# Compressed probabilities in pairs, 512-column scores, later additions and another loading of the first tiles, in a hybrid decoder layer

## The chip, the cores and the metric

The kernel runs on one core of a Trainium2 chip. The metric is the device time of one execution in microseconds, median over runs. The core has five engines with instruction streams of their own: TensorE (PE, with weight loads shown apart as PEld), VectorE (DVE), ScalarE (ACT), GpSimd (POOL) and SyncE (SP, which here only issues DMAs).

## The reference

One decoder layer on 512 tokens of width 1024: a pooling mixer and an attention with compressed and windowed keys side by side, merged by sigmoid gates, then a gated conv-MLP. What matters here, cut down:

```python
h = rms_norm(x, mix_norm_g)
u, q, kv, nsa_g, merge_g = split(h @ w_in)            # pool input, queries, 6 key/value slots, gates
gate_pool, gate_nsa = split(sigmoid(merge_g))
y_pool = pooling_mixer(u, pool_w, pool_scale) @ w_pool_out   # running means over 2, 4, 8, 16 tokens
# attention, per head h (8 heads, 2 key groups): three branches, each a softmax
#   compressed: 31 blocks of 32 tokens, through a small MLP: blk = kv[:, idx] + cmp_pe; silu(blk @ w1) @ w2
#   selected and windowed: with 512 tokens both see every earlier token
out = g0 * (p_cmp @ vc) + g1 * (p_sel @ v_sel) + g2 * (p_win @ v_win)
x = x + (gate_pool * y_pool + gate_nsa * (out @ w_nsa_out)) @ w_out
h = rms_norm(x, ffn_norm_g)
gate_pre, val = split(h @ w_up)
x = x + (silu(causal_dwconv(gate_pre)) * val) @ w_down
```

## The kernel before

Every float32 product is made of three products of rounded halves (high by high, high by low, low by high), so most weights and activations are split by a rounding copy on ACT and a subtraction on DVE, or by a DMA from POOL's queue that adds. The program isn't written in its final order: each call is recorded, and a planner (`Plan`, emitted at one line, so that every row of the profile reads L395) puts the instructions of each engine in order from its own costs and due times. PE work is recorded in two streams: `m` (the main one: projection, rotary transposes, compression, attention) and `f` (the filler: 22 "features", each 24 matmuls of 512 columns on `xh`, `xl` with weights `wf`, then the pool mixer's output products). The planner takes from `f` where `m` has to wait, so the order of `f` is free to be chosen.

The stages in time: `first()` and `round_a` (the projection to queries and keys: tiles `tr`, `av`, `sc` <- `whi`, `xh`), values (`bh`, `bl`), rotary rope and the transposes of queries and keys (`qs`, `ks` into `qt`, `kt`), compression (`kcb`, `w1`, `hid`, `kcsp`, `kcz`), attention head by head, `wno`, `wout`, then the MLP (`wup`, `wdn`, `wdz`).

The steps that the change touches:

- **The beginning.** Ten float32 matmuls of `ones` come first on PE. ACT issues the load of a small parameter tile `pr`, then does one dummy activation `warm`, which loads its table. SP issues, in this order: half of the first weights (`raw[:, :T]`), both halves of the first x tile `xr[0]`, the rest of the weights. ACT rounds the weights, then each half of x to `xh[0]`; DVE makes `xl[0]` from both halves.
- **Key transposes** (`qk_transpose`). For each block t of 128 tokens, eight transposes of queries and four of keys; three ACT copies make two layouts `KT[0, t]`, `KT[1, t]`.
- **Scores** (`scores(h, i)`). For head h and query block i there are n = i + 1 key blocks; each takes two matmuls (high and low halves of the keys) of 256 columns, 20 per head:

```python
for j in range(n):
    for s in range(2):
        PE.matmul(pt[:, j], QT[g, i][:, hh], KT[s, j][:, g], ...)
```

- **Compressed branch.** `cmp_softmax(g)` makes probabilities in three parts (high, low, high) of 32 columns in `cst`; `cmp_transpose(g, i)` transposes 96 columns of each head of group g, four transposes for each of eight (g, i); `av` multiplies them by `vst` (96 rows, 64 columns). The addition `blk + cmp_pe` (tiles `kcb` <- `kc`) is done by POOL, four times on 128x512.
- **The order of `f`.** First the two compressed features (`kv_in`: tiles `kc`), then `pool_in` and gates by turns; `mix(gi)` (three matmuls `mm<-pmh,pwh`, `mm<-pml,pwh`, `mm<-pmh,pwl`) follows one feature after the `pool_in` that it needs.

Of the kernel before, what the change touches and what calls it, by code (L numbers as in the profile page):

```python
# [2 lines left out]

# [12 lines left out]
P = 128  # L16
T = 512
# [381 lines left out]
def hybrid_layer(ctx: ExitStack, tc: tile.TileContext, xT, pos, par, cst, poolw, w1, wa, wb, wf,  # L399
# [9 lines left out]
    def f32(ap):  # L409
        return ap.bitcast(F32)  # L410
# [12 lines left out]
    def bank(tag, shape=(P, T)):  # L423
        return pl.tile(ps, shape, F32, tag, tag, {"mm": 2, "tr": 3, "av": 1, "sc": 1}[tag], psum=True)
# [66 lines left out]

    POOL.memset(ones, 1.0)
    ACT.dma_start(pr[:, 0:16], par[:, 0:16])
    ACT.activation(warm, ones[:, 0:1], AF.Square)
    pt = bank("mm")
    for i in range(10):
        PE.matmul(pt[:, 0:P], ones, ones, start=(i == 0), stop=(i == 9))

    xr, xh, xl = [None] * KD, [None] * KD, [None] * KD
    acc = page("acc")  # L500
# [10 lines left out]
    def first():  # L511
        raw, hi, low = ring("wraw"), ring("whi", F32R), ring("wlo", F32R)
        xr[0] = page("xr")
        xh[0], xl[0] = page("xh", dt=F32R), page("xl", dt=F32R)
        cuts = (slice(0, H2), slice(H2, T))
        with pl.unit():
            SP.dma_start(raw[:, :T], wa[0, :, :T])
            for c in cuts:
                SP.dma_start(xr[0][:, c], xT[0, :, c])
            SP.dma_start(raw[:, T:768], wa[0, :, T:768])  # L520
        ACT.activation(hi[:, :T], raw[:, :T], AF.Copy)
        for c in cuts:
            with pl.behind(pl.last()):
                ACT.activation(xh[0][:, c], xr[0][:, c], AF.Copy, scale=mixg[:, 0:1])
        with pl.behind(pl.last()):
            ACT.activation(hi[:, T:768], raw[:, T:768], AF.Copy)
        DVE.scalar_tensor_tensor(xl[0], xr[0], mixg[:, 0:1], f32(xh[0]), op0=ALU.mult, op1=ALU.subtract)
        DVE.tensor_sub(low[:, :768], raw[:, :768], f32(hi[:, :768]))
        for t in range(NT):
            PE.matmul(psq[t], xh[0][:, t * P:(t + 1) * P], hi[:, 0:512], start=True, stop=False)  # L530
        for t in range(NT):
            PE.matmul(pskt[:, t // 2, t % 2], xh[0][:, t * P:(t + 1) * P], hi[:, 512:768], start=t % 2 == 0, stop=False,
                      skip_group_check=True)
        wak[0] = hi, low
# [172 lines left out]
    def qk_transpose(t):  # L707
        for g in range(2):
            pt = bank("tr", (P, 4, P))
            with pl.unit():  # L710
                for i in range(4):
                    PE.transpose(pt[:, i], f32(qsp[t][g][:, i].rearrange("p a d -> p (a d)")), ident)
            QT[g, t] = page("qt", (P, 4, P), F32R)
            ACT.activation(QT[g, t], pt, AF.Copy)
        pt = bank("tr", (P, 2, 2, P))
        with pl.unit():
            for g in range(2):
                for b in range(2):
                    PE.transpose(pt[:, g, b], f32(ksp[t][:, 2 * b + g].rearrange("p a d -> p (a d)")), ident)
        KT[0, t], KT[1, t] = (page("kt", (P, 2, 2, P), F32R) for _ in range(2))  # L720
        ACT.activation(KT[0, t], pt, AF.Copy)
        ACT.activation(KT[1, t][0:64], pt[64:128], AF.Copy)
        ACT.activation(KT[1, t][64:128], pt[0:64], AF.Copy)

    rope_split(0)
    rope_split(1)
# [19 lines left out]
    pscale = R("pscale")  # L746
    yph, ypl, pooled = [], [], {}
    with pl.on("f"):
        for i in range(2):
            pt = feature(i, xh, xl)  # L750
            kc = page("kc", (P, 2, 256))
            for g in range(2):
                for q in range(2):
                    DVE.tensor_mul(kc[q * 64:(q + 1) * 64, g], pt[g * 64:(g + 1) * 64, q::2],
                                   rb[g * 64:(g + 1) * 64, q::2])
            for a in range(2):
                b = page("kcb", (P, 2, 32, 8))
                POOL.tensor_add(b.rearrange("p g n l -> p (g n) l"), kc.rearrange("p g (n l) -> p (g n) l", l=8),
                                pe[:, i, 8 * a:8 * a + 8][:, None, :].to_broadcast([P, 64, 8]))
                KC[i, a] = b  # L760
        def pool_in(gi):
            w = 2 << gi
# [36 lines left out]
        def pool_out(c):  # L799
            wh, wl = weights(wpo[c].rearrange("p a k n -> p (a k n)"), 1024)  # L800
            for f in (2 * c, 2 * c + 1):
# [3 lines left out]
                DVE.scalar_tensor_tensor(gpy[f], gpy[f], 1.0, pt, op0=ALU.add, op1=ALU.mult)  # L805
                SP.dma_start(gdr[f], gpy[f])

        pool_in(0)
        pw = page("pw", (P, 4, P))
        with pl.behind(turned[1]):  # L810
            SP.dma_start(pw, poolw)
        split(pwh, pwl, pw)
        for gi in range(1, 4):
            pool_in(gi)
            gate(thn, gi - 1, 14)
            mix(gi - 1)
        gate(thn, 3, 14)
        mix(3)
        for f in (0, 2):
            gate(gpy, f, 6)  # L820
            gate(gpy, f + 1, 6)
            pool_out(f // 2)
        gate(thn, 4, 14)
        for f in (4, 6):
            gate(gpy, f, 6)
            gate(gpy, f + 1, 6)
            pool_out(f // 2)
        for f in range(5, 8):
            gate(thn, f, 14)

    chid = []
    for i in range(2):
# [40 lines left out]
        for z in kcz.values():  # L873
            POOL.memset(f32(z), 0.0)
    pk = compress_out(1)
    vst = keep("vst", (96, 2, DH), F32R)
    for g in range(2):
        src = pk[g * 32:(g + 1) * 32, 0:64]
        for s in range(2):
            ACT.activation(vst[s * 32:(s + 1) * 32, g], src, AF.Copy, scale=0.5)  # L880
        DVE.scalar_tensor_tensor(vst[64:96, g], src, 0.5, f32(vst[g * 32:(g + 1) * 32, g]),
                                 op0=ALU.mult, op1=ALU.subtract)

    def compress_kt():
        pt = bank("tr")
# [11 lines left out]
    cps, cst_ = {}, {}  # L897
    PTc = {g: pl.tile(sb, (96, 4, T), F32R, "ptc", "ptc", 1) for g in range(2)}

    def cmp_scores(g):  # L900
        pt = bank("tr")
# [8 lines left out]
    def cmp_softmax(g):  # L910
        pt = bank("tr", (P, 4, P))
        with pl.unit():
            for hh in range(4):
                PE.transpose(pt[:, hh], cps[g][:, hh], ident)
        e = page("ce", (P, 16, 32))
        e4 = e.rearrange("p (h t) n -> p h (t n)", h=4)
        sm = keep("csm", (P, 3, 16), bufs=2)
        st = cst_[g] = keep("cst", (P, 16, 3, 32), F32R)
# [12 lines left out]
    def cmp_transpose(g, i):  # L931
        pt = bank("tr", (P, 4, P))
        with pl.unit():
            for hh in range(4):
                PE.transpose(pt[0:96, hh], f32(cst_[g][:, 4 * hh + i].rearrange("p a n -> p (a n)")), ident)
        ACT.activation(PTc[g][:, :, i * P:(i + 1) * P], pt[0:96], AF.Copy)

    Pt, PT, po, Oraw = {}, {}, {}, {}
    Oh = [page("oh", dt=F32R) for _ in range(4)]
# [2 lines left out]
    def scores(h, i):  # L942
# [1 line left out]
        n = i + 1  # L944
        pt = bank("sc", (P, 4, 2, P)) if n > 2 else bank("tr", (P, 2, 2, P))
        with pl.unit():
            for j in range(n):
                for s in range(2):
                    PE.matmul(pt[:, j], QT[g, i][:, hh], KT[s, j][:, g], start=(s == 0 and j % 2 == 0),
                              stop=(s == 1), skip_group_check=True)  # L950
# [79 lines left out]
    cmp_softmax(0)  # L1030
    scores(0, 2)
    scores(0, 3)
    extra = {(0, 2 * i + 2): (lambda i=i: cmp_transpose(0, i)) for i in range(NT)}
    extra.update({(4, 2 * i): (lambda i=i: cmp_transpose(1, i)) for i in range(NT)})
    extra[2, 6] = lambda: cmp_softmax(1)
    for h in range(H):
        def nxt(i):
# [396 lines left out]
```

## Time and profile before

| | |
|---|---|
| median of 3 runs | 698.51 us (698.43 to 698.52) |
| the profiled execution | 698.77 us, of which 697.0 us are the span of its instructions |
| PE busy | 691.3 us, 4144 matmuls |
| DVE, ACT, POOL busy | 481.1, 436.3, 103.3 us |
| granted TensorE clock | 1.0 |

Matmuls are pipelined: the duration of a row (0.39 us for 512 columns) is longer than the distance from one start to the next, and it is the distance that sets the pace. Rows of the timeline give the start, the time until the last of a group ends, the engine, the operation, the tile that is written `<-` the tiles that are read, and in brackets the idle time before it with what ended it.

### The profile page before, as it was taken

How to read it: one execution, taken by the hardware profiler on the slowest of the kernel's cores; microseconds unless marked ns; L12 is line 12 of the kernel's file. 1: busy time of each engine (PE TensorE's matmuls, PEld its weight loads, DVE VectorE, ACT ScalarE, POOL GpSimd, SP SyncE). 2: the span in 40 equal slices, each digit the busy share in tenths (PEclk: the TensorE clock that was granted, in tenths of full speed). 3: DMA queues.
4: the chain of work that ended last, by engine and by line, in shares of the span. 5: the costliest groups of instructions: out<-in, count | busy, mean ns of one | idle time of the engine just before them, and what ended most of it. 6: DMA issues, size and time to landing. Idle time of an engine off the chain costs nothing.

```text
span 697.0 us, 11326 instructions
## 1 busy us (share of the span) xinstructions
PE 691.3 (99%) x4144; PEld 612.0 (88%) x4144; DVE 481.1 (69%) x1025; ACT 436.3 (63%) x798; POOL 103.3 (15%) x127
## 2 busy tenths in 40 slices
PE   9999999999999999999999999999999999999998
PEld 8898888888888888888888899999999999999987
DVE  5768678888866653685559977777766766776542
ACT  7667568767777663443359757768677766675320
POOL 0011400010011010000013223223122112220000
PEclk9999999999999999999999999999999999999999
DMA  8577344355655558744459787879978867864141
GB/s 297 171 177 207 96 111 107 106 137 122 166 136 152 151 126 240 272 164 136 151 144 233 168 214 174 215 169 198 225 189 180 196 162 168 182 158 108 46 128 61
DMA packets 45703, 113.99 MB, mean 164 GB/s; under 512 B 5328, under 2 KB 6096, under 8 KB 45648
## 3 DMA queue, kind: packets, MB, share of 16 engines
q1 hardware_dynamic: 29664, 76.57, 34.2%
q0 software_dynamic: 15840, 36.71, 29.2%
q8 instruction: 32, 0.52, 0.3%
q14 instruction: 23, 0.19, 0.1%
q10 hardware_dynamic: 144, 0.01, 0.0%
HBM read 70.27 MB, written 6.29 MB: 110 GB/s over the span
## 4 chain that ended last, share of the span: by engine, by line
PE 97%; DVE 2%; issue 0%; ACT 0%; POOL 0%; POOLq 0%
PE mm L395 41%; PE tr L395 31%; PE sc L395 14%; PE av L395 11%; DVE kp L395 1%; DVE kc L395 0%; DVE qp L395 0%; DVE th L395 0%; DVE qs L395 0%; DVE rt L395 0%; DVE ks L395 0%; DVE pml L395 0%; DVE o L395 0%; ACT ks L395 0%; POOL ones L395 0%
## 5 line engine op out<-in xcount | busy, mean ns | idle before, releaser
L395 ACT ACTIVATE whi<-wraw 128x1024 fp32r<-128x1024 f32 (+2 forms) x97 | 98.0, 1011 | 69.5 <-issue 24.6
L395 DVE TENSOR_TENSOR wlo<-wraw,whi 128x1024 fp32r<-128x1024 f32 (+1 forms) x66 | 76.3, 1158 | 16.9 <-ACT whi L395 14.9
L395 POOL DMA_DIRECT2D wlo<-wraw x30 | 26.3, 876 | 327.5 <-ACT wlo L395 257.9
L395 PE MATMUL mm<-xh,whi 128*128 128x512 f32 x176 | 73.0, 415 | 0.1
L395 PE MATMUL mm<-xh,wlo 128*128 128x512 f32 x176 | 69.0, 392 | 0.0
L395 PE MATMUL mm<-xl,whi 128*128 128x512 f32 x176 | 68.9, 392 | 0.0
L395 PE MATMUL mm<-tl,sh 128*128 128x256 f32 x190 | 53.5, 282 | 0.0
L395 PE MATMUL mm<-th,sl 128*128 128x256 f32 x174 | 49.1, 282 | 0.0
L395 PE MATMUL mm<-th,sh 128*128 128x256 f32 x174 | 49.0, 281 | 0.0
L395 ACT ACTIVATE wlo<-wraw 128x1024 fp32r<-128x1024 f32 x30 | 31.8, 1059 | 25.5 <-PE mm L395 16.6
L395 POOL DMA_DIRECT2D sl<-r x36 | 31.1, 863 | 88.0 <-ACT sl L395 66.1
L395 ACT ACTIVATE pp<-pp,asm 128x128 f32<-128x128 f32 (+3 forms) x64 | 35.4, 556 | 9.4 <-DVE asm L395 9.3
L395 PE MATMUL sc<-yh,whi 128*128 128x512 f32 x104 | 40.5, 389 | 0.0
L395 PE MATMUL sc<-yl,whi 128*128 128x512 f32 x104 | 40.5, 389 | 0.0
L395 PE MATMUL sc<-yh,wlo 128*128 128x512 f32 x104 | 40.5, 389 | 0.0
L395 PEld LDWEIGHTS mm<-xh,wlo 128*128 128x128 f32 x176 | 33.0, 188 | 7.5
L395 DVE SCALAR_TENSOR_TENSOR ft<-fg,pr,ft 128x511 f32<-128x511 f32 (+1 forms) x44 | 32.9, 749 | 9.5 <-ACT ft L395 8.8
L395 PEld LDWEIGHTS mm<-xh,whi 128*128 128x128 f32 x176 | 33.2, 188 | 4.7 <-DVE th L395 0.5
L395 PEld LDWEIGHTS mm<-xl,whi 128*128 128x128 f32 x176 | 33.3, 189 | 4.0
L395 PEld LDWEIGHTS mm<-tl,sh 128*128 128x128 f32 x190 | 35.7, 188 | 0.4
L395 PEld LDWEIGHTS mm<-th,sh 128*128 128x128 f32 x174 | 32.7, 188 | 1.1
L395 PEld LDWEIGHTS mm<-th,sl 128*128 128x128 f32 x174 | 32.7, 188 | 0.0
(397 smaller groups left out, 2100.6 us busy)
## 6 DMA issues: line engine op xcount, KB each, us to landing
wlo<-wraw POOLq DMA_DIRECT2D x30, 512.0 KB, 4.6
wraw<-wup SPq DMA_DIRECT2D x26, 512.0 KB, 3.9
wraw<-wf SPq DMA_DIRECT2D x22, 512.0 KB, 3.4
r<-wup SPq DMA_DIRECT2D x36, 256.0 KB, 5.4
sl<-r POOLq DMA_DIRECT2D x36, 256.0 KB, 5.4
wraw<-wdn SPq DMA_DIRECT2D x16, 512.0 KB, 3.7
sl<-s POOLq DMA_DIRECT2D x18, 256.0 KB, 5.5
sl<-wraw POOLq DMA_DIRECT2D x18, 256.0 KB, 4.2
```

The lines of the kernel that those rows point to most:

```text
L395: getattr(self.real[o.eng], method)(*a, **kw)
```

## The change

- `first()`: eight matmuls of `ones` instead of ten. The second half of `xr[0]` is issued by ACT, after `pr` and before the table load; the first weights are rounded by DVE instead of ACT, and the first half of x no longer stands behind that.
- Key transposes are done for two blocks at once, per group; `KT[s, pair, g]` holds two blocks side by side, and scores use 512 columns for a pair of blocks, 256 for a single one: 12 matmuls per head.
- `cmp_softmax` makes two parts (high, low) instead of three; two heads stand side by side in 128 columns, so four calls of `cmp_transpose` of four transposes instead of eight. `PTc` holds head pairs; the values `vz` (128 rows, 128 columns, zero rows for the other head of the pair) share a tile with the probabilities.
- `kcb` is added by DVE, and stands behind the last key copy (`turned[3]`).
- `f` begins with a gate, `mix` comes one `pool_in` and two gates later, and the pool's outputs come last.

```diff
-    ACT.activation(warm, ones[:, 0:1], AF.Square)
-    for i in range(10):
+    for i in range(8):
...
             SP.dma_start(raw[:, :T], wa[0, :, :T])
-            for c in cuts:
-                SP.dma_start(xr[0][:, c], xT[0, :, c])
+            SP.dma_start(xr[0][:, cuts[0]], xT[0, :, cuts[0]])
             SP.dma_start(raw[:, T:768], wa[0, :, T:768])
-        ACT.activation(hi[:, :T], raw[:, :T], AF.Copy)
+        ACT.dma_start(xr[0][:, cuts[1]], xT[0, :, cuts[1]])
+        ACT.activation(warm, ones[:, 0:1], AF.Square)
+        DVE.tensor_copy(hi[:, :T], raw[:, :T])
         for c in cuts:
-            with pl.behind(pl.last()):
+            with pl.behind(pl.last()) if c.start else nullcontext():
                 ACT.activation(xh[0][:, c], xr[0][:, c], AF.Copy, scale=mixg[:, 0:1])
...
+        for g in range(2 if t % 2 else 0):
+            pt = bank("tr", (P, 2, 2, P))
+            with pl.unit():
+                for j in range(2):
+                    for b in range(2):
+                        PE.transpose(pt[:, j, b], f32(ksp[t - 1 + j][:, 2 * b + g]...), ident)
+            hl, lh = (page("kt", (P, 2, 2, P), F32R) for _ in range(2))
+            KT[0, t // 2, g], KT[1, t // 2, g] = hl, lh
...
-                POOL.tensor_add(b..., kc..., pe...)
+                with pl.behind(turned[3]):
+                    DVE.tensor_add(b..., kc..., pe...)
...
+        gate(thn, 0, 14)
+        kv_in(0)
+        kv_in(1)
+        gate(thn, 1, 14)
         pool_in(0)
...
+        gate(thn, 2, 14)
+        gate(thn, 3, 14)
+        pool_in(1)
+        mix(0)
...
-        ACT.activation(st[:, :, 0], e, AF.Copy)
-        ACT.activation(st[:, :, 2], e, AF.Copy)
-        DVE.tensor_sub(st[:, :, 1], e, f32(st[:, :, 0]))
+        ACT.activation(hi, e, AF.Copy)
+        DVE.tensor_sub(lo, e, f32(hi))
...
+    def cmp_transpose(g, b):
+            for q in range(2):
+                for a in range(2):
+                    PE.transpose(pt[:, q, a], f32(cst_[:, 2 * b + a, 2 * q:2 * q + 2]...), ident)
...
-            for j in range(n):
+            for j in range(0, n, 2):
+                m = min(2, n - j)
                 for s in range(2):
-                    PE.matmul(pt[:, j], QT[g, i][:, hh], KT[s, j][:, g], start=(s == 0 and j % 2 == 0),
+                    PE.matmul(pt[:, j:j + m], QT[g, i][:, hh], KT[s, j // 2, g][:, 0:m], start=(s == 0), stop=(s == 1),
...
-            PE.matmul(o[0:64], vst[:, g], PTc[g][:, h % 4], start=False, stop=False)
+            PE.matmul(o, vz[:, g, h % 2].rearrange("p s d -> p (s d)"), PTc[:, h // 2], start=False, stop=False)
```

More of the change, by code (lines that the diff above doesn't have):

```diff
@@ L1 @@
 import math
-from contextlib import ExitStack, contextmanager
+from contextlib import ExitStack, contextmanager, nullcontext
 import concourse.bass as bass
@@ L493, in hybrid_layer @@
     ACT.dma_start(pr[:, 0:16], par[:, 0:16])
-    ACT.activation(warm, ones[:, 0:1], AF.Square)
     pt = bank("mm")
-    for i in range(10):
-        PE.matmul(pt[:, 0:P], ones, ones, start=(i == 0), stop=(i == 9))
+    for i in range(8):
+        PE.matmul(pt[:, 0:P], ones, ones, start=(i == 0), stop=(i == 7))
     xr, xh, xl = [None] * KD, [None] * KD, [None] * KD
@@ L714, in qk_transpose @@
             ACT.activation(QT[g, t], pt, AF.Copy)
[L715 to L723, printed above, removed]
+        for g in range(2 if t % 2 else 0):
[3 more added lines that the diff above has]
+                    for b in range(2):
+                        PE.transpose(pt[:, j, b], f32(ksp[t - 1 + j][:, 2 * b + g].rearrange("p a d -> p (a d)")), ident)
+            hl, lh = (page("kt", (P, 2, 2, P), F32R) for _ in range(2))
+            KT[0, t // 2, g], KT[1, t // 2, g] = hl, lh
+            ACT.activation(hl, pt, AF.Copy)
+            ACT.activation(lh[0:64], pt[64:128], AF.Copy)
+            ACT.activation(lh[64:128], pt[0:64], AF.Copy)
     rope_split(0)
@@ L748, in hybrid_layer, with kv_in @@
     with pl.on("f"):
-        for i in range(2):
+        def kv_in(i):
             pt = feature(i, xh, xl)
@@ L757, in hybrid_layer @@
                 b = page("kcb", (P, 2, 32, 8))
-                POOL.tensor_add(b.rearrange("p g n l -> p (g n) l"), kc.rearrange("p g (n l) -> p (g n) l", l=8),
-                                pe[:, i, 8 * a:8 * a + 8][:, None, :].to_broadcast([P, 64, 8]))
+                with pl.behind(turned[3]):
+                    DVE.tensor_add(b.rearrange("p g n l -> p (g n) l"), kc.rearrange("p g (n l) -> p (g n) l", l=8),
+                                   pe[:, i, 8 * a:8 * a + 8][:, None, :].to_broadcast([P, 64, 8]))
                 KC[i, a] = b
@@ L812, in hybrid_layer @@
         split(pwh, pwl, pw)
[L813 to L816, printed above, removed]
+        gate(thn, 2, 14)
         gate(thn, 3, 14)
-        mix(3)
[L819 to L829, printed above, removed]
+        pool_in(1)
+        mix(0)
+        gate(thn, 4, 14)
+        gate(thn, 5, 14)
+        pool_in(2)
+        mix(1)
+        gate(thn, 6, 14)
+        gate(thn, 7, 14)
+        pool_in(3)
+        mix(2)
+        gate(gpy, 0, 6)
+        gate(gpy, 1, 6)
+        mix(3)
+        pool_out(0)
+        gate(gpy, 2, 6)
+        gate(gpy, 3, 6)
+        pool_out(1)
+        gate(gpy, 4, 6)
+        gate(gpy, 5, 6)
+        pool_out(2)
+        gate(gpy, 6, 6)
+        gate(gpy, 7, 6)
+        pool_out(3)
     chid = []
@@ L875, in hybrid_layer @@
     pk = compress_out(1)
-    vst = keep("vst", (96, 2, DH), F32R)
+    ct = keep("cst", (P, 3, T), F32R)
+    cst_ = ct[:, 0:2].rearrange("p a b -> p (a b)").rearrange("p (t h s n) -> p t h s n", t=4, h=4, s=2)
+    vz = ct[:, 2].rearrange("p (g r s d) -> p g r s d", g=2, r=2, s=2)
+    with pl.behind(turned[2]):
+        POOL.memset(f32(ct[:, 2]), 0.0)
     for g in range(2):
         src = pk[g * 32:(g + 1) * 32, 0:64]
[L879 to L882, printed above, removed]
+        for r in range(4):
+            ACT.activation(vz[r * 32:(r + 1) * 32, g, r // 2, 0], src, AF.Copy, scale=0.5)
+        for r in range(2):
+            DVE.scalar_tensor_tensor(vz[r * 64:r * 64 + 32, g, r, 1], src, 0.5, f32(vz[g * 32:(g + 1) * 32, g, 0, 0]),
+                                     op0=ALU.mult, op1=ALU.subtract)
     def compress_kt():
@@ L895, in compress_kt @@
                                AF.Copy)
-    cps, cst_ = {}, {}
-    PTc = {g: pl.tile(sb, (96, 4, T), F32R, "ptc", "ptc", 1) for g in range(2)}
+    cps = {}
+    PTc = pl.tile(sb, (P, 4, T), F32R, "ptc", "ptc", 1)
     def cmp_scores(g):
@@ L917, in cmp_softmax @@
         sm = keep("csm", (P, 3, 16), bufs=2)
-        st = cst_[g] = keep("cst", (P, 16, 3, 32), F32R)
+        hi, lo = (cst_[:, :, :, s].rearrange("p t h n -> p h t n") for s in range(2))
         DVE.tensor_add(e4, pt, C("cmask")[:, None, :].to_broadcast([P, 4, P]))
@@ L926, in cmp_softmax @@
         DVE.tensor_mul(e, e, sm[:, 2][:, :, None].to_broadcast([P, 16, 32]))
-        ACT.activation(st[:, :, 0], e, AF.Copy)
-        ACT.activation(st[:, :, 2], e, AF.Copy)
-        DVE.tensor_sub(st[:, :, 1], e, f32(st[:, :, 0]))
-    def cmp_transpose(g, i):
-        pt = bank("tr", (P, 4, P))
+        e = e.rearrange("p (h t) n -> p h t n", h=4)
+        ACT.activation(hi, e, AF.Copy)
+        DVE.tensor_sub(lo, e, f32(hi))
+    def cmp_transpose(g, b):
+        pt = bank("tr", (P, 2, 2, P))
         with pl.unit():
-            for hh in range(4):
-                PE.transpose(pt[0:96, hh], f32(cst_[g][:, 4 * hh + i].rearrange("p a n -> p (a n)")), ident)
-        ACT.activation(PTc[g][:, :, i * P:(i + 1) * P], pt[0:96], AF.Copy)
+            for q in range(2):
+                for a in range(2):
+                    PE.transpose(pt[:, q, a], f32(cst_[:, 2 * b + a, 2 * q:2 * q + 2].rearrange("p h s n -> p (h s n)")), ident)
+        ACT.activation(PTc[:, 2 * g:2 * g + 2, 2 * b * P:2 * (b + 1) * P], pt.rearrange("p q a t -> p q (a t)"), AF.Copy)
     Pt, PT, po, Oraw = {}, {}, {}, {}
@@ L946, in scores @@
         with pl.unit():
-            for j in range(n):
+            for j in range(0, n, 2):
+                m = min(2, n - j)
                 for s in range(2):
-                    PE.matmul(pt[:, j], QT[g, i][:, hh], KT[s, j][:, g], start=(s == 0 and j % 2 == 0),
-                              stop=(s == 1), skip_group_check=True)
+                    PE.matmul(pt[:, j:j + m], QT[g, i][:, hh], KT[s, j // 2, g][:, 0:m], start=(s == 0), stop=(s == 1),
+                              skip_group_check=True)
         sm = keep("asm", (P, 4, 2), bufs=4)
@@ L1032, in hybrid_layer @@
     scores(0, 3)
-    extra = {(0, 2 * i + 2): (lambda i=i: cmp_transpose(0, i)) for i in range(NT)}
-    extra.update({(4, 2 * i): (lambda i=i: cmp_transpose(1, i)) for i in range(NT)})
+    extra = {(0, 4 * b + 2): (lambda b=b: cmp_transpose(0, b)) for b in range(2)}
+    extra.update({(4, 4 * b): (lambda b=b: cmp_transpose(1, b)) for b in range(2)})
     extra[2, 6] = lambda: cmp_softmax(1)
```

## The prediction

> **What bounds the kernel now.** I read the page's busy times and chain first, then the waits of PE, then the timeline around each place that the change touches.
>
> ```profile
> PE 691.3 (99%) x4144; PEld 612.0 (88%) x4144; DVE 481.1 (69%) x1025; ACT 436.3 (63%) x798; POOL 103.3 (15%) x127
> ```
> ```profile
> PE 97%; DVE 2%; issue 0%; ACT 0%; POOL 0%; POOLq 0%
> ```
> ```profile
> PE tr L395 <- DVE rt L395: 1.3, 1, 1.3
> PE mm L395 <- POOL ones L395: 1.0, 1, 1.0
> ```
> ```profile
> 270.10 14.28 PE mm L395 x63
> ```
>
> PE is busy for 99% of the span and carries 97% of the chain that ended last; in all it waits twice by the view of waits. So each PE instruction that goes is worth its distance to the next start, and work on DVE, ACT and POOL counts only where PE ends up waiting for it. The fifth row, a piece of the chain, shows 63 filler matmuls in one stretch at the end of attention: the main stream finishes with 14 us of filler left, so a main stream that comes somewhat earlier or later is absorbed. From `wno` on, the order of PE's instructions in the built program is the same as before; all of the effect lies ahead of that.
>
> **Probabilities in pairs.** The number of `cst` transposes falls from 32 to 16. A group of four, and what follows it:
>
> ```profile
> 114.15 0.60 PE L395 MATMUL tr<-cs,cst 128*96 128x128 f32 x4
> 114.51 0.47 PE L395 MATMUL mm<-xh,whi 128*128 128x512 f32 x1
> 114.82 0.39 PE L395 MATMUL mm<-xl,whi 128*128 128x512 f32 x1
> ```
>
> Start to start, the group takes 0.36 us and the matmul behind it 0.31 instead of 0.23 (a price that the next part shows): 0.44 us per group. The new groups have 128 rows instead of 96 on the output side; the neighbouring `pp` transposes have 128 as well and I take the same price. Four groups go: −1.76 us. The product with the values keeps 512 columns and its count, so I price it at nothing. On ACT, copies disappear (two per softmax become one, and half of the `ptc` copies go), four small ones are added; nobody on PE waits for these.
>
> **512-column scores.** Per head 20 matmuls become 12: 16 of the 256-column ones become 8 of 512, 64 fewer in all.
>
> ```profile
> 94.42 3.79 PE L395 MATMUL tr<-qt,kcz 128*128 128x512 f32 x16
> 98.05 0.64 PE L395 MATMUL tr<-kt,qt 128*128 128x256 f32 x4
> ```
> ```profile
> 101.74 1.12 PE L395 MATMUL sc<-kt,qt 128*128 128x256 f32 x8
> 102.69 0.40 PE L395 MATMUL mm<-xh,whi 128*128 128x512 f32 x1
> ```
>
> Sixteen of 512 columns take 98.05 − 94.42 = 3.63 us, 0.227 each; eight of 256 take 102.69 − 101.74 = 0.95, 0.119 each. A pair costs 0.238 against 0.227: 0.011 × 64 = −0.7 us. The same columns pass through; only a small cost per instruction goes. Scores of pairs need key copies of both blocks, so the first head's can begin only after the second block's transposes; filler stands between.
>
> **The wait of 1.5 us.** The largest stall is at the query transposes of the fourth block:
>
> ```profile
> 72.08 0.39 PE L395 MATMUL mm<-xh,wlo 128*128 128x512 f32 x1
> 73.81 0.63 PE L395 MATMUL tr<-cs,qs 128*128 128x128 f32 x4 [1.35 <-DVE rt L395]
> ```
> ```profile
> 61.89 0.42 DVE L395 TENSOR_TENSOR kp<-kp,gkv 128x256 f32<-128x256 f32 x1
> ```
> ```profile
> 65.03 1.72 DVE L395 TENSOR_TENSOR kc<-mm,rb 64x256 f32<-64x256 f32 x4
> ```
> ```profile
> 66.79 0.23 DVE L395 TENSOR_TENSOR kp<-kp,rope 128x64 f32<-128x64 f32 x1
> 67.05 1.19 DVE L395 TENSOR_TENSOR kp<-kp,rt 128x64 f32<-128x64 f32 x1
> ```
> ```profile
> 69.21 0.41 DVE L395 TENSOR_TENSOR ks<-kp,ks 128x256 fp32r<-128x256 f32 x1
> ```
> ```profile
> 70.79 2.31 DVE L395 TENSOR_TENSOR kp<-kp,gkv 128x256 f32<-128x256 f32 x1
> ```
> ```profile
> 71.22 1.60 POOL L395 TENSOR_TENSOR kcb<-kc,pr 128x512 f32<-128x512 f32 x1
> ```
> ```profile
> 73.25 0.42 DVE L395 TENSOR_TENSOR qs<-qp,qs 128x256 fp32r<-128x256 f32 x1
> ```
>
> Between two starts lie 1.73 us instead of 0.23: 1.50 lost. The cause stands in DVE's rows: the same multiplication `kp<-kp,gkv` takes 0.42 us alone and 2.31 while POOL adds `kcb`. A smaller one, 128x64, had 1.19 against 0.23 under the addition before. DVE's split `qs`, queued behind both, comes 1.89 + 0.96 us late, and PE waits for it. The change takes POOL's additions away; and the features whose `kc` rows (1.72 us for four) stood ahead in DVE's queue come after a gate now, which puts one 512-column product in there instead. A product of that size is 0.69 by a row quoted next:
>
> ```profile
> 83.60 0.69 DVE L395 TENSOR_TENSOR u<-mm,rb 128x512 f32<-128x512 f32 x1 [1.06 <-PE mm L395]
> ```
> ```profile
> 77.49 1.80 ACT L395 ACTIVATE kt<-tr 128x512 fp32r<-128x512 f32 x3 [0.34 <-PE tr L395]
> ```
>
> DVE therefore gets to `qs` earlier by 1.89 + 0.96 + 1.72 − 0.69 = 3.9 us. PE arrives earlier too: in the built order 51 filler matmuls and 32 transposes stand ahead of that point instead of 60 and 36, 9 × 0.227 + 4 × 0.09 = 2.4 us. So the wait falls by 3.9 − 2.4 = 1.5 us, to nothing, and the built order leaves a margin: it puts the last steps of the third block's keys (0.23, 0.23, 0.41 by the rows) behind `qs` on DVE. I take −1.5, with 0 and −1.5 as ends.
>
> What comes late next is compression. The four `kcb` additions are on DVE now, 0.69 us each, and stand behind the last key copy on ACT. Behind them on DVE are the evictions of the second compressed feature, and PE's first `kcb` matmul waits for the first addition. ACT's copies take 0.60 each; the built order does the one that is waited for first, after PE's last key transposes. So 0.1 + 0.6 + 0.69 = 1.4 us must be covered, and nine filler matmuls, 2.0 us, stand there: no wait. If ACT did all six copies first, 3.6 us, PE would wait 2.3.
>
> **Later additions.** The pool mixer's products wait on DVE's low halves:
>
> ```profile
> 145.44 0.39 PE L395 MATMUL mm<-pmh,pwl 128*128 128x512 f32 x1
> 145.93 0.50 PE L395 MATMUL mm<-xh,whi 128*128 128x512 f32 x1
> ```
> ```profile
> 153.28 0.48 PE L395 MATMUL mm<-pmh,pwh 128*128 128x512 f32 x1
> 153.86 0.50 PE L395 MATMUL mm<-pml,pwh 128*128 128x512 f32 x1
> 154.20 0.39 PE L395 MATMUL mm<-pmh,pwl 128*128 128x512 f32 x1
> ```
>
> Over 0.227 each, these lose 0.26 + 0.35 + 0.11 = 0.7 us. With `mix` two gates later there are over 10 us between; I take −0.5, ends 0 and −0.7, since another order meets its own small waits.
>
> **The beginning.**
>
> ```profile
> 0.99 4.63 PE L395 MATMUL mm<-ones 128*128 128x128 f32 x20 [0.99 <-POOL ones L395]
> ```
> ```profile
> 1.18 0.90 SPq L395 DMA_DIRECT2D xr<-xT  x2
> ```
> ```profile
> 3.65 0.63 ACT L395 ACTIVATE whi<-wraw 128x512 fp32r<-128x512 f32 x1 [0.98 <-DMA wraw<-wa]
> ```
> ```profile
> 4.18 0.49 ACT L395 ACTIVATE xh<-xr,pr 128x256 fp32r<-128x256 f32 x1
> ```
> ```profile
> 5.28 1.74 PE L395 MATMUL tr<-whi,xh 128*128 128x512 f32 x3
> ```
> ```profile
> 5.69 0.51 ACT L395 ACTIVATE xh<-xr,pr 128x256 fp32r<-128x256 f32 x1 [1.02 <-DMA xr<-xT]
> ```
> ```profile
> 6.84 0.41 PE L395 MATMUL av<-whi,xh 128*128 128x512 f32 x1
> 7.09 0.63 PE L395 MATMUL sc<-whi,xh 128*128 128x256 f32 x4
> ```
> ```profile
> 40.80 1.05 PE L395 MATMUL mm<-diag,ones 128*128 128x128 f32 x8
> 41.61 0.38 PE L395 MATMUL mm<-bh,xh 128*128 128x280 f32 x1
> ```
>
> The 20 passes of the ten warm-up matmuls are 0.21 apart (4.29 / 20) and end at 5.28, though `xh` was there at 4.67: the first product waited for the warm-up. Sixteen passes end at 4.4. With DVE rounding weights from 3.65 and ACT free for x, the first product starts at 4.4 to 4.75. The third needs the second half of x, which lands at 5.69 now. Issued from ACT it goes out one issue, 0.45 us, sooner (two on SP take 0.90): the chain from there moves by 0.45. Nearest other bound: it could land with the first half, by 4.18, and then PE's start decides, 0.85. A third bound is below: the same passes are 0.10 apart at 40.80 (0.81 / 8), so PE is at half pace at first; three products of 512 columns take 1.56 us from 5.28, the next one 0.25, so half pace lasts until some 6.5, and 0.45 us gained at half pace is 0.2. I take −0.4, ends −0.85 and, with the rival below, +1.6.
>
> [...]
>
> **The sum.** −1.76 − 0.7 − 1.5 − 0.5 − 0.4 = −4.9 us. For waits of the new order that I can't see I add 0.5, an estimate: a third of the largest one before. That makes −4.4: from 698.77 us for the profiled execution (span 697.0 and 1.77 around it) to 694.4. The median of the runs before is 0.26 lower than the profiled one, so I predict 694.2.
>
> **The rivals.**
> *A wait takes the place of the removed one* (0.13): DVE or ACT brings `kcb`, or `kcsp` behind it, late. For it: the additions lengthen DVE's queue by 4 × 0.69, and cover is 2.0 against 1.4. Against: POOL no longer blocks DVE. Price 2.3 in place of the allowance of 0.5: −2.6, 696.0.
> *The clock comes up late* (0.07). Half pace lasted from 0.99 to about 6.5, 5.5 us of unbroken work. Now a gap opens between the warm-up's end and the second half of x. If the 5.5 us begin again at 4.6, PE is at half pace until 10.1: 3.6 us more, 1.8 lost, and with the 0.2 still gained +1.6 in place of −0.4: 696.2. [...]
> *Slower* (0.06): the main stream ends after the filler. Attention's start is pushed back by a gate ahead of compression (24 × 0.227 = 5.4 us) and by DVE's additions (2.8). Up to 14.3 us of delay the remaining filler covers it; beyond, PE idles one for one. It takes a delay of 20 us or more to be slower than before by over 1.3: at 20, 694.2 + 5.7 = 699.9. Against: the two known delays make 8.2.
> *The parts don't do what they say* (0.08): scores pace alike, the old waits return elsewhere; only the transposes and little else remain, −1.4 or less: about 697.5.
>
> **How the numbers follow.** The forecast has 0.66. All terms at their better end without the allowance (−1.76, −0.7, −1.5, −0.7, −0.85) give 693.0, and 0.3 for a score pair that gains a little more 692.7. The range is 692.7 to 697.0, which takes in the first two rivals. A measurement of this kernel tells about 0.2% from no change, 1.4 us. Faster: forecast and the first two rivals, less a little for their upper ends, 0.84; within 0.2%: 0.09; slower: 0.07.
>
> **What would show it.** Right: 32 transposes `cst` become 16 and `kt,qt` matmuls fall by 64 with 0.227 between those of 512; no wait of PE for DVE at the fourth block; no DVE operation over 1.3 us there; first product at 4.4 to 4.75. Wrong: a wait over 1 us ahead of `kcb` or `kcsp`; half pace beyond 7; less than 5 us of filler after the last `av`.

## The result, and the profile after

| | before | after |
|---|---|---|
| median, us | 698.47 (698.31 to 698.87, 6 runs) | 693.19 (692.65 to 693.89, 6 runs) |
| profiled execution, us | 698.77 | 693.21 |
| its span, us | 697.0 | 691.4 |
| PE matmuls | 4144 | 4060 |

The ratio is 0.9925, with a 95% interval of 0.9912 to 0.9938. The change is 5.28 us faster by the medians and 5.56 by the profiled executions; the forecast was 694.2.

The page of the changed kernel, busy times; then its list of waits of PE (us in total, times, longest):

```profile
PE 687.2 (99%) x4060; PEld 606.8 (88%) x4060; DVE 479.6 (69%) x1032; ACT 432.2 (63%) x795; POOL 98.3 (14%) x124
```
```profile
PE mm L395 <- POOL ones L395: 1.0, 1, 1.0
```

84 matmuls are gone: 64 of the scores, 16 `cst` transposes, 4 passes of the warm-up. Of the two waits only the first microsecond is left. The groups by shape and the timeline (start, duration) answer to the prediction's rows:

```profile
L395 PE MATMUL sc<-kt,qt 128*128 128x512 f32 x48 | 13.7, 392 | 0.0
...
L395 PE MATMUL tr<-kt,qt 128*128 128x512 f32 x16 | 5.1, 396 | 0.0
...
L395 PE MATMUL tr<-kt,qt 128*128 128x256 f32 x16 | 3.4, 294 | 0.0
L395 PE MATMUL sc<-kt,qt 128*128 128x256 f32 x16 | 3.2, 281 | 0.0
...
L395 PE MATMUL tr<-cs,cst 128*128 128x128 f32 x16 | 2.4, 272 | 0.0
```
```profile
4.83 1.65 PE L395 MATMUL tr<-whi,xh 128*128 128x512 f32 x3
...
7.11 0.40 PE L395 MATMUL tr<-whi,xl 128*128 128x512 f32 x1
...
40.06 1.05 PE L395 MATMUL mm<-diag,ones 128*128 128x128 f32 x8
...
68.96 1.03 PE L395 MATMUL tr<-cs,qs 128*128 128x128 f32 x8
...
75.53 3.82 PE L395 MATMUL tr<-kcb,w 128*128 128x62 f32 x32
...
90.73 0.33 PE L395 MATMUL tr<-cs,kcsp 64*128 64x64 f32 x2
...
108.02 0.60 PE L395 MATMUL tr<-cs,cst 128*128 128x128 f32 x4
108.38 0.48 PE L395 MATMUL mm<-xh,whi 128*128 128x512 f32 x1
108.70 0.39 PE L395 MATMUL mm<-xl,whi 128*128 128x512 f32 x1
```
```profile
264.54 14.28 PE mm L395 x63
```

The scores are 64 matmuls of 512 columns and 32 of 256, where there were 160 of 256. A group of `cst` transposes keeps its price: 0.36 to the next start and 0.32 for the matmul behind it. The fourth block's eight query transposes start at 68.96 without a wait ahead of them or a gap between them, and `kcb` isn't waited for. The last row is the same 63 filler matmuls as before, 5.56 us earlier; from there to the end nothing moves.

Where the 5.56 us lie follows from four places. The first product that reads `xl`, and `kcsp`, in the kernel before:

```profile
7.56 0.40 PE L395 MATMUL tr<-whi,xl 128*128 128x512 f32 x1
```
```profile
92.42 0.33 PE L395 MATMUL tr<-cs,kcsp 64*128 64x64 f32 x2
```

The product that reads `xl` stands at 7.11 now: 0.45 up to there. The diagonal products stood at 40.80 and stand at 40.06: 0.74 up to there, 0.29 more. But between these two places lie the same 192 matmuls in the same order, in these two kernels and in all twelve of the experiments, and no wait in PE's lists lies there. They take 33.24 us in the profile before and 32.95 in the one after, and 32.80 to 33.41 in all fourteen profiles: 32.95 also in two kernels with the old beginning (`e3_order`, `e6_kcb_dve`), 33.41 in one with the new beginning alone (`e4_front`). So these 0.29 us belong to the executions, not to the change.

`kcsp` stands at 90.73 now, 1.69 earlier: 0.95 more, though three more filler matmuls (0.68) are done by then, so 1.63 went apart from them. From `kcsp` to the filler stretch 3.87, of which 0.68 is that filler, done already; 3.19 is left.

| stretch | forecast | profiled execution |
|---|---|---|
| beginning, up to the first product with `xl` | −0.4 | −0.45 |
| the same 192 matmuls of the projection | none | −0.29 |
| wait at the fourth block | −1.5 | −1.63 |
| pairs, scores, later additions | −1.76 − 0.7 − 0.5 = −2.96 | −3.19 |
| waits of the new order | +0.5 | none seen |

The parts of the row of pairs, scores and later additions can be added up in the two traces, each matmul counted from its start to the next start. The scores take 19.49 us before and 18.79 after (−0.70), the `cst` transposes with the products of the values 4.79 and 3.28 (−1.51, without the matmul behind each group), the mixer's twelve products 3.54 and 2.88 (−0.66).

DVE's rows at the fourth block, and ACT's key copies, changed kernel:

```profile
66.47 0.75 DVE L395 TENSOR_TENSOR kp<-kp,gkv 128x256 f32<-128x256 f32 x2
...
67.44 0.76 DVE L395 TENSOR_TENSOR qs<-qp,qs 128x256 fp32r<-128x256 f32 x2 [0.21 <-ACT qs L395]
...
72.57 1.28 DVE L395 TENSOR_TENSOR kcb<-kc,pr 128x512 f32<-128x512 f32 x2
```
```profile
73.65 3.63 ACT L395 ACTIVATE kt<-tr 64x512 fp32r<-64x512 f32 x6 [0.47 <-PE tr L395]
```

Two `kp<-kp,gkv` take 0.75 together, where one had 2.31, and `qs` is done at 68.20, 0.76 before PE gets there. The first two additions are done at 73.85, before PE's `kcb` at 75.53.

### The profile page after: what moved, and what is told of

Its sections match the earlier page's. It is cut to its first block, busy times and chain, and to the rows that moved or that the text cites. A ratio compares the mean times of both kernels' runs of the same rounds, so it can differ in the third digit from the quotient of the medians.

```text
span 691.4 us, 11144 instructions
## 1 busy us (share of the span) xinstructions
PE 687.2 (99%) x4060; PEld 606.8 (88%) x4060; DVE 479.6 (69%) x1032; ACT 432.2 (63%) x795; POOL 98.3 (14%) x124
## 4 chain that ended last, share of the span: by engine, by line
PE 99%; DMA 0%; ACT 0%; DVE 0%; SPq 0%; issue 0%; ACTq 0%
PE mm L395 42%; PE tr L395 32%; PE sc L395 14%; PE av L395 11%; DMA xr<-xT 0%; ACT xh L395 0%; DVE o L395 0%; SPq L395 0%; ACTq L395 0%
## 5 line engine op out<-in xcount | busy, mean ns | idle before, releaser
L395 ACT ACTIVATE pp<-pp,asm 128x384 f32<-128x384 f32 (+3 forms) x64 | 35.4, 557 | 5.8 <-DVE asm L395 5.8
```

Of the source, the lines that this page charges most:

```text
L395: getattr(self.real[o.eng], method)(*a, **kw)
```

## The experiments

The kernel before had medians of 698.44, 698.34 and 698.26 us beside the three groups of runs.

**Each part alone.** Four kernels, each the kernel before with one part of the diff.

`e1_pairs`, with the tiles `vz`, `cst` and `PTc` that go with it:

```diff
-        for hh in range(4):
-            PE.transpose(pt[0:96, hh], f32(cst_[g][:, 4 * hh + i]...), ident)
+        for q in range(2):
+            for a in range(2):
+                PE.transpose(pt[:, q, a], f32(cst_[:, 2 * b + a, 2 * q:2 * q + 2]...), ident)
```

> The kernel before with the compressed probabilities in pairs alone. Theory (each part is worth the PE time that it removes, and the parts add up): 16 cst transposes instead of 32, 1.8 us less between the compressed scores and wno, the 1.5 us wait at the fourth block's query transposes stays; 698.5 - 1.8 = 696.7. Rival (any edit makes the planner lay out another order, and it is this that removes the waits): the 1.5 us wait changes here as well, and the time is 1 us or more away from 696.7.

Measured: 695.80 (695.41 to 697.53), ratio 0.9967 (0.9951 to 0.9983).

`e2_scores`, with the copies `KT` of two blocks:

```diff
-                    PE.matmul(pt[:, j], QT[g, i][:, hh], KT[s, j][:, g], ...
+                    PE.matmul(pt[:, j:j + m], QT[g, i][:, hh], KT[s, j // 2, g][:, 0:m], ...
```

> The kernel before with key copies of two blocks and 512-column scores alone. Theory: 64 fewer matmuls at 0.011 us, 0.7 us less: 697.8; PE's wait at the fourth block stays at about 1.5 us. Rival (order by chance): the wait changes, 1 us or more away from 697.8.

Measured: 696.99 (695.51 to 698.55), ratio 0.9984 (0.9974 to 0.9994).

`e3_order`, both of these, with the other steps in the new order too:

```diff
-                POOL.tensor_add(b..., kc..., pe...)
+                with pl.behind(turned[3]):
+                    DVE.tensor_add(b..., kc..., pe...)
...
+        gate(thn, 0, 14)
+        kv_in(0)
+        kv_in(1)
```

> The kernel before with kcb on DVE behind the last key copy and the new order of the filler, nothing else. Theory: the wait of 1.5 us goes, the waits of the pool mixer's products (0.7 us) go: 696.3. No DVE operation of the rotation over 1 us. Rival (order by chance): 1 us or more away from 696.3, with waits elsewhere.

Measured: 696.25 (695.95 to 696.47), ratio 0.9970 (0.9959 to 0.9982).

`e4_front`:

```diff
-    for i in range(10):
+    for i in range(8):
...
+        ACT.dma_start(xr[0][:, cuts[1]], xT[0, :, cuts[1]])
-        ACT.activation(hi[:, :T], raw[:, :T], AF.Copy)
+        DVE.tensor_copy(hi[:, :T], raw[:, :T])
```

> The kernel before with the new beginning alone (eight warm-ups, half of x from ACT's queue, first weights rounded by DVE). Theory: the first product that reads xl starts at 7.1 instead of 7.56 and the values' first matmul 0.7 us earlier, as in the changed kernel; 697.8. Rival (what is gained at the beginning is waited for later, at the next weights or at the fourth block): PE is 0.45 us early at first and no more than 0.2 at wno; 698.3.

Measured: 699.19 (698.39 to 699.95), ratio 1.0010 (1.0001 to 1.0020).

Only `e3_order` came out as priced. The four shifts (−2.64, −1.45, −2.19, +0.75) add up to −5.53, close to the −5.28 of the whole, but not because the parts are independent. In `e1_pairs` and `e2_scores` the 1.5 us wait is gone as well, though neither takes POOL's additions away (`e1_pairs` adds a memset to POOL's queue there, `e2_scores` regroups the key transposes beside it). Timeline of `e1_pairs`, DVE and POOL:

```profile
67.00 0.41 DVE L395 TENSOR_TENSOR kp<-kp,gkv 128x256 f32<-128x256 f32 x1
67.33 1.39 DVE L395 TENSOR_TENSOR qp<-qp,gq 128x128 f32<-128x128 f32 x1
...
70.05 0.42 DVE L395 TENSOR_TENSOR kp<-kp,gkv 128x256 f32<-128x256 f32 x1
```
```profile
65.78 2.78 POOL L395 TENSOR_TENSOR kcb<-kc,pr 128x512 f32<-128x512 f32 x2 [1.26 <-DVE kc L395]
```

POOL still adds, and holds up one row of DVE, `qp<-qp,gq` (1.39 us instead of 0.28). But in this layout its two additions are over at 68.56, and DVE has time left ahead of the fourth block's `qs`: the multiplications take 0.41 and 0.42. In exchange `e1_pairs` waits 1.2 us in the MLP, whose code it doesn't touch (timeline, PE; the profiled execution, 696.75, is the second slowest of its five), and `e4_front` has two new waits, with 0.5 us left of the old one (list of waits):

```profile
524.27 0.39 PE L395 MATMUL mm<-th,sh 128*128 128x256 f32 x1 [1.18 <-ACT u L395]
```
```profile
PE mm L395 <- DVE th L395: 0.7, 1, 0.7
PE mm L395 <- ACT u L395: 0.6, 1, 0.6
PE tr L395 <- DVE qs L395: 0.5, 1, 0.5
```

So an edit anywhere makes the planner lay out other queues, and the waits follow the layout. The next kernels hold that apart from the parts.

**The layout alone.** `e5_replan` is the kernel before with one constant of the planner, `e12_replan_after` the changed kernel with another.

```diff
-RESERVE = 3
+RESERVE = 4
```

> The kernel before with one constant of its planner changed (RESERVE 4 for 3, pages held back), no part of the change in it: the same instructions of the computation, issued in another order (on PE a few stretches of filler stand elsewhere, on DVE and ACT more). Theory of the parts (each part brings what its rows were priced at, wherever it stands): with nothing taken away the time stays within 0.5 us of before, 698.0 to 698.9, and the 1.5 us wait for DVE at the fourth block's query transposes is still there. Rival, the plan (which waits there are is set by the order that the planner happens to lay out): the time moves by over 0.7 us, and the wait at the fourth block goes or shrinks without any of the change.

Measured: 699.27 (698.84 to 699.63), ratio 1.0015 (1.0006 to 1.0024). The waits of PE, from its list:

```profile
PE tr L395 <- DVE rt L395: 1.3, 1, 1.3
...
PE tr L395 <- DVE pt L395: 0.6, 1, 0.6
```

Half of each theory came: the old wait stays, as the first had it, and the time moves by 0.9 us without any part of the change, as the rival had it, with a new wait of 0.6 us in the list.

```diff
-LANDS = (0.8, 0.8, 1.2, 1.2, 2.0, 2.0)
+LANDS = (1.0, 1.0, 1.0, 1.0, 1.0, 1.0)
```

> The whole change with one constant of its planner changed (LANDS at 1.0 throughout, the time that it allows a transfer): PE's order is the same instruction by instruction, ACT and DVE issue theirs in another order. Theory, PE alone sets the time and its order is enough: 693.2 with 0.3 either way. Rival, the order on ACT and DVE brings waits of its own: slower by 0.5 to 2.5 us, 693.7 to 695.7, with waits of PE for DVE or ACT in the trace.

Measured: 695.92 (694.55 to 698.62), ratio 0.9975 (0.9964 to 0.9986): 2.7 us slower than the changed kernel, with PE's order the same to the instruction. The profiled execution (694.55) is the fastest of its runs; PE and ACT in it:

```profile
491.33 0.39 PE L395 MATMUL mm<-th,sh 128*128 128x256 f32 x1 [0.88 <-ACT u L395]
```
```profile
489.70 1.05 ACT L395 ACTIVATE whi<-wraw 128x1024 fp32r<-128x1024 f32 x1
490.65 0.36 ACT L395 ACTIVATE fg<-av 128x256 f32<-128x256 f32 x1
490.92 0.37 ACT L395 ACTIVATE u<-mm 128x256 f32<-128x256 f32 x1
```

ACT rounds 1024 columns of later weights (1.05 us) ahead of the small `u` for which PE waits. The same place in the changed kernel, where `u` stands ahead of the longer work and PE doesn't wait:

```profile
488.89 0.38 ACT L395 ACTIVATE u<-mm 128x256 f32<-128x256 f32 x1
489.17 0.63 ACT L395 ACTIVATE sl<-r 128x512 fp32r<-128x512 f32 x1
```

The rival held in kind, with a median a little above its 695.7: the order on ACT and DVE counts though PE carries the chain. Between the two profiled executions lie 1.3 us (694.55 against 693.21), and this wait is 0.9 of them. What made its other runs up to 4 us slower no profile shows; the three slowest (697.64 to 698.62) have a granted clock of 0.997 or 0.998, the others 0.999 or 1.0.

**What removed the 1.5 us wait.** The prediction said: POOL's additions go. Three kernels take the two halves of that part apart. `e6_kcb_dve` is the kernel before with the first three lines of `e3_order`'s diff alone:

> The kernel before with one line of the change alone: the four additions to the compression keys on DVE behind the last key copy, not on POOL; the order of the filler steps as before. Theory of the parts: no POOL work beside DVE's key rows any more, so kp by gkv takes 0.42 us, the wait of 1.5 us goes and nothing else does: 697.0. Rival, a wait takes its place: the additions come late behind DVE's queue, with the feature steps still ahead of them, and PE waits ahead of kcb by up to 2.3 us: 698 to 699. Rival, the plan: any value from 696.5 to 699, with new waits elsewhere.

Measured: 697.67 (697.04 to 698.29), ratio 0.9991 (0.9981 to 1.0000).

`e9_steps_only` is the kernel before with the rest of `e3_order`'s diff alone, the steps in the new order:

> The kernel before with the order of the filler's steps alone (two gates ahead of the compressed features, mix two gates later); the additions to the compression keys stay on POOL. From the whole change with POOL's additions (693.32) I take it that the later place of the feature steps removes the 1.5 us wait, not the change of engine: then this measures what both together did, 696.25, within 0.4, and no DVE operation on the key rows takes over 1.3 us. Rival, the engine counts after all in this plan: the wait stays in part, 697.3 to 698.4. Rival, the plan: new waits of up to 1.3 us elsewhere, anything from 696 to 699.

Measured: 696.13 (695.34 to 696.28), ratio 0.9971 (0.9960 to 0.9982).

`e8_pool_kcb` is the whole change with the additions back on POOL:

```diff
-                with pl.behind(turned[3]):
-                    DVE.tensor_add(b..., kc..., pe...)
+                POOL.tensor_add(b..., kc..., pe...)
```

> The whole change, but the additions to the compression keys stay on POOL, as before. Theory of the parts: POOL's additions again fall beside DVE's key rows, which take 1.2 and 2.3 us, and PE waits 1.5 us ahead of the fourth block's query transposes: 694.7. Rival, the later place of the feature steps is what counts: with them behind two gates of filler POOL's additions fall behind those rows, no DVE operation there takes over 1.3 us, and the time is that of the whole change, 693.2 with 0.3 either way.

Measured: 693.32 (692.88 to 693.59), ratio 0.9930 (0.9915 to 0.9944).

Moving the additions to DVE alone does remove the wait, but the medians move by 0.7 us only. `e6_kcb_dve`'s list has two waits at the mixer:

```profile
PE mm L395 <- ACT pmh L395: 0.6, 1, 0.6
...
PE mm L395 <- DVE pml L395: 0.3, 1, 0.3
```

The first, ahead of a mixer product that reads `pmh`, is new. The second isn't: the mixer's twelve products take 3.49 us from start to start, 3.54 in the kernel before.

The order of the steps alone gives what both gave together (696.13 against 696.25), and in the whole change the engine makes no difference (693.32 against 693.19, ranges overlapping). In `e9_steps_only` the additions start only when the key rows are over; DVE, then POOL:

```profile
68.18 0.42 DVE L395 TENSOR_TENSOR kp<-kp,gkv 128x256 f32<-128x256 f32 x1
...
70.00 0.76 DVE L395 TENSOR_TENSOR qs<-qp,qs 128x256 fp32r<-128x256 f32 x2 [0.47 <-ACT qs L395]
...
71.01 1.72 DVE L395 TENSOR_TENSOR kc<-mm,rb 64x256 f32<-64x256 f32 x4
```
```profile
72.82 2.55 POOL L395 TENSOR_TENSOR kcb<-kc,pr 128x512 f32<-128x512 f32 x2 [6.80 <-DVE kc L395]
```

`kc`, the features' copies, come behind `qs` now, so POOL can't start earlier than 72.8. So either half alone removes the wait; the order of the steps brings what the part is worth, and the move to DVE is not needed for it.

In the kernel before POOL also issues a DMA (`wlo<-wraw`, at 70.60 for 0.90 us) while `kp<-kp,gkv` takes 2.31. In `e6_kcb_dve` such an issue runs from 71.54 without any addition, and DVE's two `qs` at 71.58 keep their 0.76 us. So it is the addition that counts.

**The beginning.** `e7_no_front` is the whole change with `e4_front`'s diff undone:

> The whole change but the beginning, which stays as it was before (ten warm-up matmuls, both halves of x on SP, first weights by ACT). Theory of the parts: the beginning's 0.74 us that the trace of the changed kernel shows up to the diagonal products is lost: 693.9. Rival, the plan (the beginning alone measured +0.75): the beginning is worth nothing in the end or costs, 692.4 to 693.3.

Measured: 693.51 (693.20 to 693.75), ratio 0.9932 (0.9916 to 0.9949). The beginning is worth some 0.3 us by the medians, less than the runs' own spread, so neither theory is confirmed. In this kernel's profile the first product with `xl` stands at 7.11, where the changed kernel has it too. `e10_warm4` and `e11_warm10` are the changed kernel with

```diff
-    for i in range(8):
+    for i in range(4):      # e11_warm10: range(10)
```

> The whole change with four warm-up matmuls (8 passes) instead of eight; everything behind them in the same order on every engine. PE then idles from about 2.7 to 4.8 us. Theory of the clock as the prediction's rival has it (half pace ends only after some stretch of unbroken work): half pace from 4.8 until 8.2 to 11.6, which loses 0.9 to 2.6 us: 694.1 to 695.8. Rival, the step to full pace comes at a time of its own, whatever runs before it: the first product starts at 4.7 to 4.9 as before and full pace begins between 4.3 and 6.6: 693.2 with 0.4 either way.

Measured: 694.24 (693.54 to 694.58), ratio 0.9944 (0.9932 to 0.9956).

> The whole change with ten warm-up matmuls (20 passes), as in the kernel before; two ACT rows change places behind them, nothing else. Where the warm-up is at half pace to its end it ends at 5.28 and holds the first product back by 0.45 us against 4.83, of which half counts where full pace begins in it. Theory, the warm-up's length sets the start: +0.2 to +0.4 us, 693.4 to 693.6. Rival, by the clock an unbroken warm-up brings the step to full pace forward (at 4.3 to 4.6 in four executions with ten matmuls, at 6.3 to 6.6 in all three with eight): equal or better, 692.5 to 693.2.

Measured: 693.02 (692.45 to 693.53), ratio 0.9930 (0.9917 to 0.9943). The first rows of PE in `e10_warm4`, `e11_warm10` and `e9_steps_only` (which has the beginning of the kernel before):

```profile
0.99 2.08 PE L395 MATMUL mm<-ones 128*128 128x128 f32 x8 [0.99 <-POOL ones L395]
4.82 1.65 PE L395 MATMUL tr<-whi,xh 128*128 128x512 f32 x3 [1.75 <-ACT xh L395]
...
6.69 1.06 PE L395 MATMUL sc<-whi,xh 128*128 128x256 f32 x4
7.55 0.46 PE L395 MATMUL tr<-whi,xl 128*128 128x512 f32 x1
```
```profile
5.29 1.18 PE L395 MATMUL tr<-whi,xh 128*128 128x512 f32 x3
6.30 0.40 PE L395 MATMUL av<-whi,xh 128*128 128x512 f32 x1
```
```profile
0.99 3.95 PE L395 MATMUL mm<-ones 128*128 128x128 f32 x20 [0.99 <-POOL ones L395]
4.70 0.71 PE L395 MATMUL tr<-whi,xh 128*128 128x512 f32 x2
```

With four warm-up matmuls the four 256-column `sc` products, 0.12 apart at full pace, take 0.86 from 6.69 to 7.55, 0.21 each: half pace lasts until some 7.6, later than in any of the other thirteen profiles (6.8 at the latest). That is the direction in which the clock rival points, but short of the 8.2 that was expected at least: no run shows half pace until 8.2 or 11.6, and from which numbers the two were taken the expectation doesn't say. By the medians the kernel is 1.05 us slower than with eight; the trace shows 0.44 of it, the first product with `xl` at 7.55 instead of 7.11. This trace is of the fastest of its five runs, and with one profile it stays open how much is due to the shorter warm-up and how much to the execution (see the last section). Ten measured the same as eight; that it be slower by 0.2 to 0.4 did not come.

No kernel tried beats the changed one by more than the runs' spread; with ten warm-up matmuls, or with the additions on POOL, it is the same.

## Why the prediction was right

The size came out of counts: what the prediction took from rows as instructions that go, or as idle time that goes, was found again in the trace, and the term that held it back was the allowance.

- **Probabilities in pairs and 512-column scores.** −1.76 and −0.7 stand. The trace has 32 → 16 transposes at the same price per group, and 64 matmuls fewer for the scores. The sums from start to start give −1.51 without the matmuls behind the groups, −0.70 for the scores and −0.66 for the mixer, for which −0.5 had been taken. The kernels with pairs of blocks have 18.77 to 18.89 us of scores in seven traces, those without 19.30 to 20.05 in seven. No time of a run isolates the 0.7: `e2_scores` also lost the old wait and met others.
- **Later additions.** The mixer's rows weren't read quite rightly. Of the three losses only those at 153.28 and 153.86 lie between the mixer's products. The matmul at 145.93 is a filler one, whose weight load waited for another row of DVE:

```profile
145.93 0.19 PEld L395 LDWEIGHTS mm<-xh,whi 128*128 128x128 f32 x1 [0.53 <-DVE th L395]
```

- **The wait of 1.5 us.** Its size was right and its carrier half right. DVE's blocked rows are the cause: `kp<-kp,gkv` takes 2.31 us beside POOL's second addition, here and in `e5_replan`, where the wait stays, and 0.41 to 0.43 everywhere else. Not every row beside an addition is held up: in `e1_pairs`, with two from 65.78 to 68.56, `qp<-av,small` at 66.07 keeps its 0.68 us and `kp<-kp,gkv` at 67.00 its 0.41, while `qp<-qp,gq` at 67.33 takes 1.39. What decides between them no run shows. But that the change takes POOL's additions away was not needed: the features' later place does it alone, which the prediction had counted only as a help to DVE's queue (1.72 less 0.69).
- **What comes late next.** No wait for `kcb`, but not by the sum worked out. The first two additions run from 72.57 to 73.85 on DVE, and ACT's six key copies only begin at 73.65: `behind` places the additions in the planner's order, and on the chip they don't wait for the copies. So no chain of 1.4 us had to be covered.
- **The beginning.** −0.4 against −0.45 in the two traces; the other 0.29 of the 0.74 up to the diagonal products is the pace of the same 192 matmuls. That the 0.45 came is partly luck. With the old beginning the first product with `xl` starts between 6.78 and 7.56 in eight profiles (mean 7.20), and the kernel before has the latest; with the new one it starts between 6.83 and 7.19 in four (mean 7.04). So the traces show some 0.2 us for the edit, and the two medians 0.3. The first product started at 4.83, outside the 4.4 to 4.75 named, because x was later than supposed: ACT's `xh` waited for its DMA until 4.27 and takes 0.5 for each half. Its two halves follow each other, 0.91 together, so the second had landed by 4.68, 1.0 earlier than before and not 0.45. The nearer bound was true there, but PE's start then decides, and it moved by 0.45 and not by 0.85. Half pace ended by 6.6, not beyond 7, so the clock rival did not come at eight matmuls.
- **The allowance of 0.5** is the mis-sized term: behind the beginning no new wait over 0.2 us is in the changed kernel's trace. Without it the forecast is 693.7. It was not idle caution: `e5_replan` and `e12_replan_after` show that a layout can cost 0.9 and 2.7 us by the medians (0.6 and 0.9 as waits in the profiles), so that this layout came out well is luck as far as the prediction goes.
- **The slower rival** has no trace: all 63 filler matmuls are still there at the end of attention.

## What to carry to other kernels

Price a removed instruction by the distance between the starts around it, and expect to find that gain again in full where PE never waits (−2.96 us were priced here, −3.19 found). A removed wait belongs to the layout as much as to the edit: with a planner, run the unchanged kernel with another constant once, to see how far the time moves by layout alone (0.9 us here), before crediting a part. Compare also a stretch in which the change leaves every instruction as it was: what differs there (0.29 us over 192 matmuls here) is the size of what a single pair of profiles can't tell. When one engine's long operation stretches another's (0.42 us to 2.31 here), look first whether the step that starts it can simply come later; it may be worth as much as moving it to another engine (696.13 us by the later place alone here, 697.67 by the move alone).

## What the runs showed of the hardware that was not expected

**The step to full pace came at another time in each execution.** With the same ten warm-up matmuls the passes of `e9_steps_only` (twenty in 4.70 − 0.99 = 3.71 us) are 0.21 apart until 4.1 and 0.11 after, by their single starts, while those of the kernel before keep 0.21 to the end (4.29 us) and products run at half pace up to about 6.6. Over eight executions with that beginning full pace came between 4.1 and 4.7 in five and between 6.3 and 6.8 in three; with eight matmuls between 5.5 and 6.7 in four, with four at some 7.6 in one. The first product's start (4.70 to 5.29 in those eight) and the first half microsecond of a comparison of these kernels hang on this. With the same ten matmuls the earliest and the latest step lie some 2.5 us apart; what sets it no run shows. Whether the short gap after eight matmuls makes it later, four executions don't settle. The granted clock doesn't show it; a window of the kernel before, where the passes are 0.21 apart (length, PE busy, granted clock, DMA share, GB/s):

```profile
2.00:3.00 1.00, 1.00 (x7) 1.00 0.79 261
```

**The same 280-column products had two paces.** In the changed kernel and in `e11_warm10`, where the same instructions stand in the same order on PE:

```profile
42.02 0.30 PE L395 MATMUL mm<-bh,xl 128*128 128x280 f32 x1
42.15 0.30 PE L395 MATMUL mm<-bh,xh 128*128 128x280 f32 x1
```
```profile
41.59 0.29 PE L395 MATMUL mm<-bl,xh 128*128 128x280 f32 x1
41.72 0.29 PE L395 MATMUL mm<-bh,xl 128*128 128x280 f32 x1
```

They are 0.133 us apart in the one and 0.128 in the other; over the 96 of that stretch it makes 0.5 us, of the same size as the whole beginning. `e10_warm4` had the faster pace too, all other profiled executions the slower. The 192 matmuls of the projection ahead of them differ too, 32.80 to 33.41 us, but the two paces don't go together: `e11_warm10` has 32.80 there and `e10_warm4` 33.31. What decides it no run shows.
